# Stick-breaking scores of two heads in two PSUM banks, the recurrence's chain in one bank, and its bonus by one 128x128 product per pair of heads

## The chip, the cores and the metric

One core of one Trainium2 chip runs the whole kernel in a single launch. The metric is the device time of one execution in microseconds (us). A time is compared as the median of several runs; before the change this is 1360.16 us (three runs, 1359.88 to 1361.38). The profile is of one further execution.

The engines are named as in the profile: PE is TensorE (matrix products; PEld are its weight loads), DVE is VectorE, ACT is ScalarE, POOL is GpSimd, SP issues most of the DMAs.

## The reference, cut to what matters

The program computes two transformer blocks on a sequence of 512 tokens with 1024 features. The change lies in the first block's mixing layer, which has two parts of 8 heads with 64 features each. The second half of the first block (a routed mixture of 32 experts) and the second block (attention with windows) are not touched.

```python
# stick-breaking attention, by blocks of 128 queries
z = einsum('bhqd,bhkd->bhqk', qb, kb) * scale          # keys 0 .. end of the block
log_rest = where(strict, log_sigmoid(-z), 0.0)
suffix = cumsum(log_rest, reverse=True) - log_rest
weights = where(strict, exp(log_sigmoid(z) + suffix), 0.0)
outs.append(einsum('bhqk,bhkd->bhqd', weights, vb))
...
# RWKV-7 recurrence, one step per token, per head
state = state * w + (state @ -kk) (kk * a)^T + v k^T
out = state @ r
...
bonus = sum(r_h * k_h * r_k, axis=-1, keepdims=True) * v_h
out = (group_norm(out) + bonus) * g
```

## The kernel before, in words

Most tensors of the mixing layer hold the 64 features of two heads in 128 partitions and the 512 tokens in columns. So a "pair" p (0 to 3) is two heads, and a half hf (0 or 1) is two pairs. The dense projections (`fm`, `vjob`, `wo_mm`; lines 213 to 215) are products of split weights: high part, low part and the cross term, each 128x512 or 128x256.

The recurrence is done by chunks of 64 tokens (8 chunks, `NCH`). `rw_dense(hf)` projects and prepares a half; `rwkv(hf)` runs `chunks` (products `xt` inside a chunk), `inverse` (a triangular inverse on DVE, common to the two pairs), `front_a` and `front_b` (transposes, then the matrices Rt and Mt of each chunk), `chain(p)` and `rest(p, po)` (normalisation, the bonus, the gate).

`chain(p)` has two parts. First come products that need no state: for each chunk and head one into the bank `po` (line 678) and one into the bank `pst` (line 681). Then DVE turns `pst` into the start values St (line 685). After that there are the steps: for chunk c the product Mt x St goes into `pst` (line 691), DVE makes the next state St of it (line 692), and the product Rt x St is accumulated on top of what lies in `po` (line 694). At the end ACT copies `po` into O (line 703), and `rest` works on O.

The bonus is computed in two products. `bonus()` (line 509) sums r*k*r_k over the features of each head with the four-column matrix `hrk` (line 513, tile `bsp`, 4x512), and DVE copies the sums into `nb` (line 514). Later `front_b` spreads the sums over the 64 features with the constant `hT` (line 659, tile `pbn`), and DVE multiplies by v into `bvo` (line 661).

The stick-breaking part is `sb(p)`. For each query block i (0 to 3, with N = 128(i+1) keys) and head h: `s0` makes the scores (line 786, tile `sbz`, K = 64 rows of the array, since a head has 64 features), two sigmoids on ACT (788, 790), masks on POOL (793), a running product on DVE (797) and a product (798); `s1` transposes the weights on PE (806, tile `sbw`) and ACT copies them (808); `s2` multiplies by the values (818, tile `sbo`). The heads go one after the other, and the score tile has one bank, `pw`.

PSUM has eight banks here: two of the tag `pa` (dense products), two of the tag `pb` (taken in turn by almost everything else), and one each of `pw`, `so`, `po` and `pst`. A product into a bank waits until the engine that read the previous contents is done.

The order of the work is set in two steps. The program is written as generators: `blend` and `mix` interleave the recurrence (`mixing`) with a `filler` (value projections, the second half's `rw_dense`, then for each pair the query and key projections and `sb`, and the first part of the output projection `wo`) by tables of estimated costs (`CR`, `SW`, `SU`). Then a scheduler of the language lays out each engine's queue, within limits, by its own estimates. Each engine executes its queue in that order, so an instruction that waits holds all behind it.

## Time and profile before

| | |
|---|---|
| median of the runs | 1360.16 us (1359.88 to 1361.38) |
| the profiled execution, its own time | 1356.27 us |
| its span, first to last instruction | 1354.6 us |
| PE busy | 1268.5 us (94%) |
| DVE busy | 726.2 us (54%) |
| ACT busy | 482.2 us (36%) |
| POOL busy | 233.2 us (17%) |
| mean granted TensorE clock | 0.959 |

Times in the profile are us from the start of the span. "Busy" counts the time in which an engine has an instruction; products are pipelined, so consecutive ones overlap in the rows and what one costs is the distance from its start to the start of the next. [...] The mixing layer fills the span up to about 440 us, the choice of experts goes to 476 us, the experts to about 740 us, and the second block the rest.

### The profile page before, as it was taken

Reading aid. Unit: us, or ns where it says so; the run is one execution under the profiler, and the core shown is the slowest. Engines: PE = TensorE matmul, PEld = TensorE weight load, DVE = VectorE, ACT = ScalarE, POOL = GpSimd, SP = SyncE. Lnnn points to the kernel's source line nnn. Section 1 sums busy time; section 2 is a strip of 40 time slices with the busy share of each in tenths; the row PEclk is TensorE's granted clock in tenths of the full one; section 3 lists DMA queues with packets and bytes.
Section 4 is the critical chain, followed back from the end, with each engine's and each line's share of the span. In section 5 each row is a group of like instructions: output and inputs, shape, how many; then the busy total and the mean of one; then the engine's idle time right before and its main releaser. Section 6 shows DMA issues by size and latency. Waiting matters only on the chain.

```text
span 1354.6 us, 22340 instructions
## 1 busy us (share of the span) xinstructions
PE 1268.5 (94%) x9018; PEld 984.4 (73%) x9018; DVE 726.2 (54%) x1654; ACT 482.2 (36%) x1003; POOL 233.2 (17%) x318
## 2 busy tenths in 40 slices
PE   7999999999989599999996899999899999999998
PEld 5778765667567355555554888888899887888888
DVE  6468566866556524443446546666544457422362
ACT  5424432544313111111113355557344564322231
POOL 2230152322420311111001322211032100000000
PEclk9979999989789699999999799999999999999999
DMA  5211100011428699999950331203321132322232
GB/s 187 74 47 63 48 32 32 32 63 48 140 78 328 227 403 372 406 397 417 401 202 1 120 106 63 86 33 99 93 89 68 53 106 64 124 93 79 93 130 74
DMA packets 41820, 188.79 MB, mean 139 GB/s; under 512 B 10887, under 2 KB 13353, under 8 KB 24560
## 3 DMA queue, kind: packets, MB, share of 16 engines
q1 hardware_dynamic: 30800, 173.93, 33.7%
q0 software_dynamic: 4448, 10.87, 2.8%
q10 hardware_dynamic: 6464, 2.52, 0.8%
q8 instruction: 73, 1.20, 0.4%
q14 instruction: 35, 0.29, 0.1%
HBM read 183.54 MB, written 7.95 MB: 141 GB/s over the span
## 4 chain that ended last, share of the span: by engine, by line
PE 50%; issue 7%; ACT 3%; DVE 2%; DMA 1%; POOL 1%; DVEq 0%; ACTq 0%; POOLq 0%
PE tm L213 7%; PE tm L214 6%; PE tm L215 6%; PE gu L1232 5%; PE fm L215 4%; PE fm L213 4%; PE fm L214 4%; PE pd L1253 3%; PE cb L1268 3%; PE az L1544 2%; ACT Pb L1555 1%; PE pbT L1761 1%; PE qT L1502 1%; PE oa L1643 1%; PE paT L1629 1%
## 5 line engine op out<-in xcount | busy, mean ns | idle before, releaser
L213 PE MATMUL tm<-wh,ah 128*128 128x256 f32 x800 | 231.1, 289 | 5.3 <-ACT vb L1669 5.3
L215 PE MATMUL tm<-wh,al 128*128 128x256 f32 x800 | 226.7, 284 | 0.0
L214 PE MATMUL tm<-wl,ah 128*128 128x256 f32 x800 | 226.4, 283 | 0.3 <-DVE wl L205 0.3
L205 DVE TENSOR_TENSOR wl<-w,wh 128x1024 fp32r<-128x1024 f32 (+1 forms) x124 | 144.2, 1164 | 147.8 <-ACT wh L204 147.6
L204 ACT ACTIVATE wh<-w 128x1024 fp32r<-128x1024 f32 (+1 forms) x124 | 124.2, 1002 | 275.6 <-PE tm L214 93.2
L213 PEld LDWEIGHTS tm<-wh,ah 128*128 128x128 f32 x800 | 151.6, 189 | 12.2 <-ACT vb L1669 5.5
L214 PEld LDWEIGHTS tm<-wl,ah 128*128 128x128 f32 x800 | 151.8, 190 | 0.8 <-DVE wl L205 0.6
L215 PEld LDWEIGHTS tm<-wh,al 128*128 128x128 f32 x800 | 151.3, 189 | 1.1 <-issue 1.0
L280 POOL TENSOR_TENSOR qss<-qss,nhalf 128x4 f32<-128x4 f32 x60 | 63.7, 1075 | 198.7 <-DVE qss L275 198.5
L213 PE MATMUL u<-xh,wh 128*128 128x512 f32 x176 | 75.8, 431 | 4.6 <-ACT xh L365 4.1
L1272 DVE TENSOR_TENSOR hres<-hres,cb 128x512 f32<-128x512 f32 x72 | 48.9, 686 | 54.3 <-PE cb L1268 54.2
L214 PE MATMUL u<-xl,wh 128*128 128x512 f32 x176 | 75.0, 426 | 1.8 <-DVE xl L366 1.8
L213 PE MATMUL fm<-ah,wh 128*128 128x512 f32 x192 | 76.0, 396 | 0.1
L215 PE MATMUL fm<-ah,wl 128*128 128x512 f32 x192 | 75.9, 395 | 0.1
L214 PE MATMUL fm<-al,wh 128*128 128x512 f32 x192 | 75.9, 395 | 0.0
L215 PE MATMUL u<-xh,wl 128*128 128x512 f32 x176 | 73.3, 416 | 1.5 <-DVE wl L205 1.5
L1253 PE MATMUL pd<-ed,hTs 128*64 128x512 f32 x256 | 62.0, 600 | 2.3 <-ACT hTs L1245 2.1
L1232 PE MATMUL gu<-eg,xgT 128*64 128x256 f32 x512 | 63.1, 384 | 0.3 <-DVE xgT L1224 0.3
L1268 PE MATMUL cb<-yh,C 128*128 128x512 f32 x128 | 55.9, 437 | 6.0 <-DVE C L1258 4.9
L1232 PE MATMUL gu<-eu,xgT 128*64 128x256 f32 x512 | 61.2, 380 | 0.0
L1235 ACT ACTIVATE hm<-gu 128x256 f32<-128x256 f32 x16 | 6.2, 384 | 148.5 <-PE hT L1243 102.2
L1232 PEld LDWEIGHTS gu<-eg,xgT 128*64 128x64 f32 x512 | 37.6, 138 | 21.8 <-issue 4.9
(404 smaller groups left out, 2527.8 us busy)
## 6 DMA issues: line engine op xcount, KB each, us to landing
w<-in_w_dram SPq DMA_DIRECT2D x33, 1024.0 KB, 4.8
eg<-in_exp_w_gate_dram SPq DMA_DIRECT2D x32, 1024.0 KB, 11.4
eu<-in_exp_w_up_dram SPq DMA_DIRECT2D x32, 1024.0 KB, 17.0
ed<-in_exp_w_down_dram SPq DMA_DIRECT2D x32, 1024.0 KB, 9.9
w<-in_wi_dram SPq DMA_DIRECT2D x22, 512.0 KB, 3.5
w<-in_wo_dram SPq DMA_DIRECT2D x8, 512.0 KB, 3.4
w<-in_wo_dram SPq DMA_DIRECT2D x4, 1024.0 KB, 4.9
xT<-in_xT_dram SPq DMA_DIRECT2D x4, 512.0 KB, 6.4
```

Of the source, the lines that this page charges most:

```text
L204: i = nc.scalar.activation(hi, src, AF.Copy)
L205: j = nc.vector.tensor_tensor(lo, src, hi.bitcast(F), op=OP.subtract)
L213: mm(out, lh, rh, start=first, stop=False)
L214: mm(out, lh, rl, start=False, stop=False)
L215: mm(out, ll, rh, start=False, stop=last)
L280: nc.gpsimd.tensor_tensor(out, out, e if len(out.shape) == 2 else e.rearrange("p (a b) -> p a b", b=out.shape[2]), op=OP.pow)
L1232: nc.tensor.matmul(ph[es, c0:c0 + 256], xt[:, c, es], EW[n, 2 * q + k][:, c, :], start=(c == 0), stop=(c == 7))
L1253: nc.tensor.matmul(pd[es, :], hT[:, c, es], EW["d", 2 * q + k][:, c, hf * 512:(hf + 1) * 512], start=(c == 0), stop=(c == 1))
L1268: nc.tensor.matmul(ps, C[:, i * 128:(i + 1) * 128], y[:, hf * 512:(hf + 1) * 512], start=(n == 0), stop=(n == 2 * len(ys) - 1))
L1272: tt(hv, hv, ps, op=OP.add)
L1502: nc.tensor.transpose(ps[:, i * 128:(i + 1) * 128], sc[:, i, :], eye)
L1544: nc.tensor.matmul(pz[j][:, off:off + k1 - k0], qt[rows, i * 128:(i + 1) * 128], kt[rows, k0:k1], start=True, stop=True)
```

## The change

1. Scores: with h = 0, `s0` now issues the score products of both heads, one into the bank `pw` and one into the bank `pst`. Head 0 uses rows 0 to 63 of the array and head 1 rows 64 to 127. The rest of `s0` is as before, head by head.
2. The chain: the state-free products go into two tiles of the tag `pb`, first all `pst` products (line 677 of the changed kernel) and then all `pso` products (line 683), and ACT copies `pso` into O at once. In the steps, both Mt x St (columns 0 to 63, line 691) and Rt x St (columns of chunk c, line 694) go into the one bank `po`, without accumulation. At the end DVE adds `po` to O (line 696). So `chain` no longer uses the bank `pst`.
3. The bonus: a 128x128 block matrix of ones, `own`, is filled by POOL at the start (three memsets). For each pair POOL scales it with r_k (line 513, tile `ownrk`), one product (line 515, tile `bsp`, now 128x512) sums over the features and spreads the sums at once, and DVE multiplies by v into `bvo` (line 517), in `bonus()` and no longer in `front_b`. The products `pbn`, the copies `nb`, the four `hrk` instructions and the constant `hT` (256 of 976 columns of the first block of constants) are gone.

```diff
-for _n, _w in (("xmask", 128), ("hind", 8), ("hT", 256), ("e0", 520), ("eye2", 64), ("ustr", 128), ("tok", 8), ("i16", 8), ("io512", 512)):
+for _n, _w in (("xmask", 128), ("hind", 8), ("e0", 520), ("eye2", 64), ("ustr", 128), ("tok", 8), ("i16", 8), ("io512", 512)):
...
-    hT = np.zeros((4, 2, 128), np.float32)
-            hT[2 * p + h, p, 64 * h:64 * h + 64] = 1
-    put("hT", hT.reshape(4, 256))
...
-        nb = [a_("nb", [4, 512], bufs=2) for _ in range(2)]
...
-        hrk = a_("hrk", [128, 4, 4])
-        for p in range(4):
-            ts(hrk[:, p, :], hind[:, p % 2, :], self.pc("rw_r_k", p), None, op0=OP.mult)
+
+        own = a_("own", [128, 128])
+        nc.gpsimd.memset(own, 0.0)
+        for h in range(2):
+            nc.gpsimd.memset(own[64 * h:64 * h + 64, 64 * h:64 * h + 64], 1.0)
+        bvs = [None] * 4
...
             def bonus():
-                bsp = self.pb("bsp")
                 for q in range(2):
-                    nc.tensor.matmul(bsp[0:4, :], hrk[:, 2 * hf + q, :], kt[q], start=(q == 0), stop=(q == 1))
-                nc.vector.tensor_copy(nb[hf][0:4, :], bsp[0:4, :])
+                    p = 2 * hf + q
+                    z = el("ownrk", [128, 128])
+                    nc.gpsimd.tensor_tensor(z, own, self.pc("rw_r_k", p).to_broadcast([128, 128]), op=OP.mult)
+                    bsp = self.pb("bsp")
+                    nc.tensor.matmul(bsp, z, kt[q], start=True, stop=True)
+                    bvs[p] = self.t(PB, "bvo", [128, 512], bufs=4)
+                    tt(ch(bvs[p]), ch(bsp), rqv[p][:, :, 128:192], op=OP.mult)
             late_bonus.append(bonus)
             if hf == 0:
                 jobs += [(lambda: first, fm(0, lora_w)[1]), fm(1, lora_g)]
...
                         nc.tensor.matmul(p1[hs, c * 64:(c + 1) * 64], W[0:64, c, h, 0:64], XT[0:64, pp, c, h, 0:64], start=True, stop=True)
                 tt(Rt, p1.rearrange("p (c t) -> p c t", t=64), rqv[p][:, :, 0:64], op=OP.add)
                 yield CR[hf][3]
-                pbn = self.pb("pbn")
-                nc.tensor.matmul(pbn, self.c("hT")[0:4, pp * 128:(pp + 1) * 128], nb[hf][0:4, :], start=True, stop=True)
-                bv = rw_("bvo", [128, 512], bufs=2)
-                tt(ch(bv), ch(pbn), rqv[p][:, :, 128:192], op=OP.mult)
-                tiles[p] += [Rt, Mt, bv]
-                yield CR[hf][3]
+                tiles[p] += [Rt, Mt]
                 if p % 2:
                     self.half = hf + 1
             def chain(p):
                 pp = p % 2
-                BK, W, Rt, Mt, _ = tiles[p]
+                BK, W, Rt, Mt = tiles[p]
                 St = cc_("St")
-                po = self.p1("po", "po")
-                pst = self.p1("pst", "pst")
+                O = dd_("O", [128, NCH, 64])
                 heads = [slice(64 * h, 64 * h + 64) for h in range(2)]
-                for c in range(NCH):
-                    o = slice(c * 64, (c + 1) * 64)
-                    for h, hs in enumerate(heads):
-                        nc.tensor.matmul(po[hs, o], XT[:, pp, c, h, 0:64], W[:, c, h, 64:128], start=(c == 0), stop=False)
-                    if c < NCH - 1:
-                        for h, hs in enumerate(heads):
-                            nc.tensor.matmul(pst[hs, o], BK[:, c, hs], W[:, c, h, 64:128], start=True, stop=True)
-                    if c == 3:
-                        yield CR[hf][4]
                 n = NCH - 1
+                pst = self.pb("pst")
+                for c in range(n):
+                    for hs in heads:
+                        nc.tensor.matmul(pst[hs, c * 64:(c + 1) * 64], BK[:, c, hs], W[:, c, hs.start // 64, 64:128], start=True, stop=True)
                 tt(St[:, 1:NCH, :], ch(pst)[:, 0:n, :], pcd[:, p, 0:n, None].to_broadcast([128, n, 64]), op=OP.mult)
                 yield CR[hf][4]
+                pso = self.pb("pso")
+                for c in range(NCH):
+                    for h, hs in enumerate(heads):
+                        nc.tensor.matmul(pso[hs, c * 64:(c + 1) * 64], XT[:, pp, c, h, 0:64], W[:, c, h, 64:128], start=True, stop=True)
+                nc.scalar.activation(O, ch(pso), AF.Copy)
+                yield CR[hf][4]
+                po = self.p1("po", "po")
                 for c in range(1, NCH):
-                    o = slice(c * 64, (c + 1) * 64)
                     if c < n:
                         for hs in heads:
-                            nc.tensor.matmul(pst[hs, o], Mt[hs, c, :], St[hs, c, :], start=True, stop=True)
-                        stt(St[:, c + 1, :], pst[:, o], pcd[:, p, c:c + 1], St[:, c + 1, :], op0=OP.mult, op1=OP.add)
+                            nc.tensor.matmul(po[hs, 0:64], Mt[hs, c, :], St[hs, c, :], start=True, stop=True)
+                        stt(St[:, c + 1, :], po[:, 0:64], pcd[:, p, c:c + 1], St[:, c + 1, :], op0=OP.mult, op1=OP.add)
                     for hs in heads:
-                        nc.tensor.matmul(po[hs, o], Rt[hs, c, :], St[hs, c, :], start=False, stop=(c == n))
+                        nc.tensor.matmul(po[hs, c * 64:(c + 1) * 64], Rt[hs, c, :], St[hs, c, :], start=True, stop=True)
                     yield CR[hf][4]
-                return po
-            def rest(p, po):
+                tt(O[:, 1:NCH, :], O[:, 1:NCH, :], ch(po)[:, 1:NCH, :], op=OP.add)
+                return O
+            def rest(p, O):
                 pp = p % 2
-                O = dd_("O", [128, NCH, 64])
-                nc.scalar.activation(O, po.rearrange("p (c t) -> p c t", t=64), AF.Copy)
                 st = a_("gst", [128, NCH], bufs=2)
                 nc.vector.tensor_reduce(st, O, axis=AX.X, op=OP.add)
                 ts(st, st, 1.0 / 64, None, op0=OP.mult)
...
-                bv = tiles[p][4]
+                bv = bvs[p]
...
             def s0(i, h):
                 N = 128 * (i + 1)
-                hs = slice(64 * h, 64 * h + 64)
-                pz = self.p1("sbz", "pw")
-                nc.tensor.matmul(pz[:, 0:N], qk[p // 2][hs, 2 * (p % 2), i * 128:(i + 1) * 128], qk[p // 2][hs, 2 * (p % 2) + 1, 0:N], start=True, stop=True)
+                if h == 0:
+                    st["z"] = [self.p1("sbz", b) for b in ("pw", "pst")]
+                    for z, r in zip(st["z"], (slice(0, 64), slice(64, 128))):
+                        nc.tensor.matmul(z[:, 0:N], qk[p // 2][r, 2 * (p % 2), i * 128:(i + 1) * 128], qk[p // 2][r, 2 * (p % 2) + 1, 0:N], start=True, stop=True)
+                pz = st["z"][h]
                 sm = s2_("sm")
                 nc.scalar.activation(sm[:, 0:N], pz[:, 0:N], AF.Sigmoid, scale=-0.125)
                 sp = s2_("sp")
```

The change moves instructions, since it changes the code's order and the scheduler lays the queues out again. Three places follow. A "[waits ...]" names the engines whose progress the row needs.

PE, the score products of pair 1, blocks 0 to 2 (`u` are dense projections, `sbw` transposes of the weights, `sbo` products with the values, `obT` transposes of pair 0's output). Before:

```order
L786 MATMUL sbz<-qk 128x128 [waits DVE_49]
L214 MATMUL u<-xl,wh 128x512
...
L786 MATMUL sbz<-qk 128x128 [waits Activation_49]
...
L786 MATMUL sbz<-qk 128x256 [waits Activation_49]
L806 MATMUL sbw<-ident,sp 128x128 [waits DVE_49,Activation_49]
L818 MATMUL sbo<-vs,wt 128x64 [waits PE_49]
...
L786 MATMUL sbz<-qk 128x256 [waits Activation_49]
```

Now:

```order
L786 MATMUL sbz<-qk 128x128 [waits DVE_49]
L786 MATMUL sbz<-qk 128x128
L212 MATMUL u<-xh,wl 128x512
...
L786 MATMUL sbz<-qk 128x256 [waits Activation_49] x2
L807 MATMUL sbw<-ident,sp 128x128 [waits DVE_49,Activation_49]
L819 MATMUL sbo<-vs,wt 128x64 [waits PE_49]
L210 MATMUL u<-xh,wh 128x512
L786 MATMUL sbz<-qk 128x384 [waits Activation_49]
L819 MATMUL sbo<-vs,wt 128x64 [waits Activation_49]
L786 MATMUL sbz<-qk 128x384 [waits Activation_49]
```

The two products of 128 and of 256 columns stand side by side now; between those of 384 columns another product still stands. Over the four pairs of heads, 10 of the 16 pairs of products are neighbours: four of 128 columns, three of 256, none of 384, three of 512.

PE, two steps of the chain of pair 3 (`wo` is the output projection). Before:

```order
L691 MATMUL pst<-St,Mt 64x64 [waits DVE_49]
L691 MATMUL pst<-St,Mt 64x64
L694 MATMUL po<-St,Rt 64x64 x2
L214 MATMUL wo<-wl,oh 128x512
L215 MATMUL wo<-wh,ol 128x512
L213 MATMUL wo<-wh,oh 128x512
L818 MATMUL sbo<-vs,wt 128x64 [waits Activation_49]
L818 MATMUL sbo<-vs,wt 128x64 x3
L214 MATMUL wo<-wl,oh 128x512
L691 MATMUL pst<-St,Mt 64x64 [waits DVE_49]
```

Now:

```order
L691 MATMUL po<-St,Mt 64x64 x2
L211 MATMUL wo<-wl,oh 128x512
L212 MATMUL wo<-wh,ol 128x512
L210 MATMUL wo<-wh,oh 128x512
L694 MATMUL po<-St,Rt 64x64 [waits DVE_49]
L694 MATMUL po<-St,Rt 64x64
L691 MATMUL po<-St,Mt 64x64 x2
L211 MATMUL wo<-wl,oh 128x512
```

The wait for DVE stood at Mt and stands now at Rt, and the other products stand between Mt and Rt of one step instead of between Rt of one step and Mt of the next.

POOL, the end of the mixing layer: the normalisation of pair 3's recurrence (`O`, `gs`) and of pair 3's stick-breaking output (`sbs`, `on`). Before:

```order
L707 TENSOR_TENSOR O<-O,gst 128x512 [waits DVE_49,Activation_49]
L280 TENSOR_TENSOR sbs<-sbs,nhalf 128x8 [waits DVE_49]
L829 TENSOR_TENSOR on<-on,sbs 128x512 [waits PE_49,Activation_49,Pool_49]
L280 TENSOR_TENSOR gs_3463<-gs_3463,nhalf 128x8 [waits DVE_49]
L716 TENSOR_TENSOR O<-O,gs_3463 128x512 [waits Activation_49,Pool_49]
```

Now:

```order
L277 TENSOR_TENSOR sbs<-sbs,nhalf 128x8 [waits DVE_49]
L830 TENSOR_TENSOR on<-on,sbs 128x512 [waits Activation_49,Pool_49]
L705 TENSOR_TENSOR O<-O,gst 128x512 [waits DVE_49]
L277 TENSOR_TENSOR gs_3452<-gs_3452,nhalf 128x8 [waits DVE_49]
L714 TENSOR_TENSOR O<-O,gs_3452 128x512 [waits Activation_49,Pool_49]
```

The two instructions of the stick-breaking output moved ahead of the recurrence's first one.

## Rows read from the trace of the kernel before

**Rows 1.** Four stretches: length, busy time of each engine, PEclk, DMA share, GB/s.

```profile
220.00:356.00 136.00, 127.49 (x1074) 90.64 (x1071) 98.17 (x185) 64.38 (x137) 46.65 (x105) 0.94 0.16 53
356.00:374.00 18.00, 18.00 (x100) 10.44 (x101) 6.98 (x14) 3.26 (x6) 2.13 (x5) 0.53 0.47 165
374.00:440.00 66.00, 59.74 (x337) 47.76 (x337) 40.80 (x62) 17.01 (x26) 9.31 (x9) 0.95 0.56 208
476.00:680.00 204.00, 201.95 (x1317) 116.90 (x1315) 80.29 (x135) 26.39 (x51) 21.45 (x22) 1.00 0.97 399
```

**Rows 2.** Timeline, PE (start, duration, what): three score products, each with its successor.

```profile
340.92 0.48 PE L786 MATMUL sbz<-qk 64*128 64x128 f32 x2
341.33 0.33 PE L681 MATMUL pst<-W,bk 128*64 128x64 f32 x2
...
303.11 0.70 PE L786 MATMUL sbz<-qk 64*128 64x256 f32 x2
303.74 0.43 PE L633 MATMUL wu<-W,T 64*64 64x128 f32 x4
...
320.72 1.12 PE L786 MATMUL sbz<-qk 64*128 64x512 f32 x2
321.77 0.44 PE L806 MATMUL sbw<-ident,sp 128*128 128x128 f32 x2
```

**Rows 3.** Timeline, PE: two products on different array rows and banks.

```profile
159.00 0.69 PE L473 MATMUL yw<-lora,w2a 64*128 64x512 f32 x1
159.01 0.69 PE L475 MATMUL ya<-lora,w2a 64*128 64x512 f32 x1
...
159.53 0.59 PE L473 MATMUL yw<-lora,w2a 64*128 64x512 f32 x1
...
160.06 0.28 PE L678 MATMUL po<-W,hres 128*64 128x64 f32 x2
```

**Rows 4.** Timeline, PE: the bonus's products, each with the row behind.

```profile
92.23 1.88 PE L513 MATMUL bsp<-kt,hrk 128*4 128x512 f32 x4
94.04 0.37 PE L541 MATMUL xt<-rqv,bk 64*128 64x128 f32 x1
...
155.07 1.12 PE L659 MATMUL pbn<-nb,cstxmask 4*128 4x512 f32 x2
156.12 0.34 PE L678 MATMUL po<-W,hres 128*64 128x64 f32 x4
...
359.36 2.07 PE L659 MATMUL pbn<-nb,cstxmask 4*128 4x512 f32 x2
361.36 0.47 PE L818 MATMUL sbo<-vs,wt 128*128 128x64 f32 x1
```

**Rows 5.** Single lines of DVE and ACT: count, ns min/median/max.

```profile
L514 DVE COPY nb<-bsp x2: 671/675/679, 94.4 to 205.9; 4x512 f32<-4x512 f32 x2
...
L661 DVE TENSOR_TENSOR bvo<-pbn,rqv x4: 690/690/693, 156.2 to 361.5; 128x512 f32<-128x512 f32 x4
...
L685 DVE TENSOR_TENSOR St<-pst,pcd x4: 611/617/625, 161.8 to 362.7; 128x448 f32<-128x448 f32 x4
...
L703 ACT ACTIVATE O<-po x4: 593/595/599, 178.9 to 378.1; 128x512 f32<-128x512 f32 x4
```

**Rows 6.** The chain: line 692 on DVE; one step, PE then DVE.

```profile
L692 DVE SCALAR_TENSOR_TENSOR St<-pst,pcd,St x24: 257/282/288, 165.7 to 376.7; 128x64 f32<-128x64 f32 x24
...
329.69 0.33 PE L691 MATMUL pst<-St,Mt 64*64 64x64 f32 x4
...
330.07 0.28 DVE L692 SCALAR_TENSOR_TENSOR St<-pst,pcd,St 128x64 f32<-128x64 f32 x1 [1.25 <-PE pst L691]
```

**Rows 7.** Timeline, POOL and then PE, end of the mixing layer.

```profile
383.84 1.64 POOL L280 TENSOR_TENSOR sbs<-sbs,nhalf 128x8 f32<-128x8 f32 x1 [3.01 <-DVE sbs L275]
385.56 1.04 POOL L829 TENSOR_TENSOR on<-on,sbs 128x512 f32<-128x512 f32 x1
...
389.38 1.98 PE L722 MATMUL oT<-ident,O 64*64 64x64 f32 x32 [3.77 <-POOL O L716]
```

## The prediction

> **What bounds the kernel now.** I read the page of the profile first: PE is busy 94% of the span and is most of the chain that ended last. An average over stages says little, so next came busy time by stretches [rows 1]. In the stretch of the stick-breaking work, 220 to 356 us, PE is busy for 127.5 of 136.0 us, while DVE is at 98 and ACT at 64: PE sets the pace, with 8.5 us in which it waits for something. In the last part of the mixing layer, 374 to 440 us, it is busy for 59.7 of 66 us. [...] Behind the mixing layer, in the experts (476 to 680 us), PE is busy for 201.95 of 204 us. The change touches nothing there, so what the mixing layer gains should reach the end: the expert loads start when buffers of the mixing layer come free, and move with it.
>
> So the question is how many us of PE's queue the change takes out before 440 us, and what it puts on paths that PE waits for.
>
> **The scores.** A product of scores alone occupies PE from its start to the next start: 0.41 us for 128 columns, 0.63 for 256, 1.05 for 512 [rows 2] (0.84 for 384, by the same slope). It uses 64 of the array's 128 rows. What two such products cost together when they use different rows and different banks is already in this kernel: lines 473 and 475, 512 columns each, start 0.01 us apart, and their second passes too (each of these products is two instructions). Both are done in 160.06 - 159.00 = 1.06 us, the price of one [rows 3]. So where two score products are neighbours in PE's queue, one of them is free; where another product stands between, nothing is gained. Ten pairs are neighbours: 4 x 0.41 + 3 x 0.63 + 3 x 1.05 = 6.7 us. In two of the three pairs of 512 columns the second product has a wait for ACT of its own; if it is late there, those two give nothing, and the sum is 4.6. I take 6.7, because ACT is busy for less than half of this stretch [rows 1].
>
> **The bonus.** The four products `pbn` go: 1.05 us each at the full clock, and the last, in the slow stretch, 2.00 [rows 4]: 3 x 1.05 + 2.00 = 5.2 us. The four products `bsp` before take about 0.9 us each (92.23 to 94.04 for two) [rows 4]; the new ones are also four products with 512 columns, so at most at the price of a `pbn`, 0.15 us more each: 0.6 us. DVE loses two copies of 0.675 us; its four products by v of 0.69 us stay, but now two of them stand in `bonus()` where one copy stood, ahead of the inverse [rows 5]: 0.7 us later there, once per half. During the inverse PE has projections to do, so I count half of the 1.4 us, with 0 and 1.4 as ends. POOL's four multiplications of 128x128 are not in the trace. Each is bounded by nothing and by the 1.04 us of a 128x512 one [rows 7]; POOL is busy for a third of the stretch [rows 1], so I count nothing, with 2 us as the other end (two of them stand ahead of work that PE's `xt` products wait for). The constants' shorter load and the three memsets at the start: nothing.
>
> **The chain.** The number of products is the same. ACT's copy of O (0.595 us) leaves the end of the chain, and DVE's addition takes its place (448 columns; line 685 has that shape, 0.617 us) [rows 5]: no difference. What changes is the waiting. A step is Mt x St on PE, then 0.28 us on DVE, and from PE's start to DVE's end it takes at least 330.07 + 0.28 - 329.69 = 0.66 us [rows 6]. Before, Rt of the same step and then projections covered this; now the projections alone do. In the changed order, 22 of the 24 steps have other products between Mt and Rt worth 0.6 us or more by starts in the timeline, so I count 0.5 us. Splitting Mt from Rt makes one more change of the array's shape per chain, and taking `pst` and `pso` each in one go makes fewer. The price of such a change comes from rows 2: from 128 to 512 columns the cost grows by 0.64 us for 384 columns, so 128 columns are 0.21 us, and 0.20 of the 0.41 is the visit itself, about 0.1 us on either side. In PE's whole queue of the mixing layer there are 15 fewer changes of shape than before, while the terms above already contain 28 (two for each of ten score products and four `pbn`). So 13 come in anew elsewhere: +1.3 us.
>
> [...] By the rows a step's reading by DVE is covered by other products, in whatever bank it lies [rows 6]. [...]
>
> **The end of the mixing layer.** PE waits 3.77 us there for the normalised O of pair 3, which POOL finishes [rows 7]. In POOL's new order two instructions of the stick-breaking output, 1.64 + 1.04 = 2.7 us, come ahead of this path, while the last values are done earlier in PE's queue. I count 0.5 us, between 0 and 2.7.
>
> **The sum.** Gains 6.7 + 5.2 = 11.9. Losses 0.6 + 0.7 + 0.5 + 1.3 + 0.5 = 3.6. That leaves 8.3 us on PE's path. Of the freed time some turns into longer waits in the stretch where PE already waits for 8.5 us; I round to 8. The profiled execution has a span of 1354.6 us and a time of 1356.3, so 1.7 us lie around the span; it is 3.9 us under the median of the runs. The same 8 us off the median: 1360.2 - 8.2 = **1352.0 us** (and about 1348 for an execution like the profiled one). With the ends of the terms: best, no losses but 1.3, 10.6 us, so 1349.6; worst, 4.6 + 5.2 - (0.6 + 1.4 + 2 + 2 + 1.3 + 2.7) = -0.2, so no change.
>
> **The rivals.**
>
> *The score pairs give nothing* (either they do not overlap, or ACT, POOL and DVE behind them set the pace, so that PE only waits longer). For: 8.5 us of waits are there already, and the masks on POOL and the running products on DVE stay in their old number. Against: rows 3. Then 11.9 - 6.7 - 3.6 = 1.6 us of gain stay, and with the two changes of shape per free pair still paid, about 1; with fewer losses up to 4. Time 1357.5, half of this case within 0.2%. Chance 0.18.
>
> *The clock follows.* The 18 us at half clock cost about 9 us. With denser work the stretch could stay at full clock: 1352 - 9 = 1343. For: the slow pieces before stand where many small products and waits stand. Chance 0.10. The opposite, a new slow piece that takes the gain back: 1361, chance 0.06.
>
> *The one bank decides, and it is slower.* If in each of the 24 steps PE stands still for the whole 0.66 us, that is 15.8 us, and the four additions of 0.62 us at the chains' ends 2.5 us. Gains of 8.3 against 18.3: 10 us slower, 1370; with half of the steps uncovered 1362. It becomes slower than before from about 0.25 us per step on. For: the scheduler's estimates set the order, and products on the chip can be shorter than it thinks. Against: before, PE's queue stood after the same kind of cover, and DVE was done 0.3 to 1 us ahead of the next Mt in most steps. Chance 0.14.
>
> **How the numbers follow.** The forecast has the rest, 0.52; its own range is 1348 to 1356. A measurement of this kernel can tell some 0.2% (2.7 us) from no change. Faster: 0.52 + 0.10 + half of 0.18 = 0.71. Same: 0.09 + 0.06 = 0.15. Slower: 0.14. The range for 8 in 10 takes in the clock's gain and the case without pairs, and leaves out most of the slower case: 1343 to 1362.
>
> **What would show it.** In the profile after: score products of two heads that start 0.01 us apart, and both done in the price of one; no `pbn`; line 692 at 0.28 us and no idle time of PE ahead of line 694; the state-free products in two blocks; the idle time ahead of `oT` still 3 to 6 us; the end of the mixing layer, and with it the experts' start, some 8 us earlier, with the stretches behind unchanged. The forecast is wrong if neighbours do not overlap, if idle time ahead of line 694 or of the transposes `sbw` has grown by several us, or if the pieces at half clock before 480 us differ from before by more than 10 us in sum.

## The result and the profile after

The changed kernel takes 1340.35 us (median of four runs, 1338.84 to 1345.2) against 1360.02; the ratio is 0.9858, interval 0.984 to 0.9876. That is 19.7 us less where 8 were forecast: 7.7 us below the forecast's own range (1348 to 1356) and 2.7 us below the wide one (1343 to 1362). Four executions over 1.5% above the fastest of their kernel (1360.97 and 1368.02 us in e12, 1361.06 and 1368.38 us in e14) are slow ones and stand outside all ratios, medians and averages below. The profiled execution of the changed kernel, 1345.2 us, is the longest of the four, as that of before (1356.3) is a short one: the two profiles are only 11 us apart.

Four stretches of the changed kernel answer to [rows 1] (length, busy time of PE, PEld, DVE, ACT and POOL with counts, PEclk, DMA share, GB/s); each is moved to where the same work lies now. The second line is a fifth stretch, around a piece at half clock.

```profile
212.00:349.00 137.00, 121.54 (x1041) 89.80 (x1038) 101.28 (x189) 61.93 (x133) 45.67 (x102) 0.94 0.16 54
338.00:345.00 7.00, 6.27 (x49) 4.80 (x49) 4.53 (x7) 0.89 (x4) 3.49 (x10) 0.57 0.11 45
349.00:374.00 25.00, 24.23 (x251) 18.26 (x246) 16.27 (x29) 8.27 (x17) 6.87 (x13) 1.00 0.51 190
374.00:428.00 54.00, 48.46 (x262) 39.10 (x262) 33.01 (x49) 14.04 (x21) 5.61 (x6) 0.94 0.61 226
464.00:668.00 204.00, 201.96 (x1315) 116.95 (x1313) 80.56 (x136) 26.38 (x51) 21.44 (x22) 1.00 0.97 399
```

The experts are as before, 201.96 of 204 us; the mixing layer ends some 12 us earlier. In the stretch of the scores PE waits for 15.5 us instead of 8.5, and the piece at half clock behind it (17.00 of the 18 us in [rows 1]) is gone; another, of 7 us, stands at 337.

The score pairs and the new bonus on PE, in the timeline (start, duration, what):

```profile
238.33 1.13 PE L786 MATMUL sbz<-qk 64*128 64x512 f32 x4
239.39 0.55 PE L807 MATMUL sbw<-ident,sp 128*128 128x128 f32 x3
...
93.24 1.88 PE L515 MATMUL bsp<-kt,ownrk 128*128 128x512 f32 x4
95.05 1.16 PE L544 MATMUL xt<-rqv,bk 64*128 64x128 f32 x8
```

Two score products of 512 columns (four instructions) take 239.39 - 238.33 = 1.06 us together, one alone took 1.05 [rows 2]; the new `bsp` takes 0.9 us, as the old one [rows 4].

From the distances of PE's starts I made a ledger for each profile, up to the first product behind the mixing layer (427.7 us before, 415.5 after). It has three parts: work at the price of the full clock (time at half clock counted half, as eight products `xt` that take 1.09 us at 197.93 us in before, at the full clock, take 2.00 at 200.33 us, at the half), what the half clock adds, and idle time over 0.15 us.

| us | before | after |
|---|---|---|
| scores | 23.4 | 16.6 |
| bonus | 7.7 | 3.7 |
| chain | 18.7 | 18.6 |
| other products | 314.2 | 314.5 |
| added by the half clock | 30.7 | 22.6 |
| idle | 33.0 | 39.4 |

Work is 10.5 us less, waits are 6.4 us more, and 8.1 us come from the clock. The waits of PE from 219 to 352 us (us in total, times, longest), first before, then after:

```profile
PE sbw L806 <- DVE sp L798: 3.2, 4, 1.7
PE bkT L590 <- DVE zo L724: 2.1, 1, 2.1
PE sbw L806 <- ACT oT L837: 1.0, 1, 1.0
```

```profile
PE sbw L807 <- DVE sp L799: 7.2, 6, 2.4
PE oT L720 <- POOL O L714: 4.0, 1, 4.0
PE oT L720 <- POOL I L797: 1.7, 1, 1.7
PE sbw L807 <- ACT sp L791: 1.5, 1, 1.5
```

The granted clock in the pieces at half clock between 190 and 400 us (the same columns), first before, 48 us in all, then after, 27 us:

```profile
199.00:206.00 7.00, 7.00 (x23) 3.05 (x23) 1.63 (x4) 0.00 (x0) 1.19 (x1) 0.51 0.00 0
233.00:243.00 10.00, 9.73 (x27) 6.29 (x27) 7.26 (x20) 3.31 (x10) 3.13 (x11) 0.51 0.01 3
281.00:288.00 7.00, 7.00 (x21) 4.61 (x20) 5.00 (x6) 2.17 (x4) 1.54 (x3) 0.51 0.49 160
356.00:373.00 17.00, 17.00 (x94) 9.93 (x93) 6.44 (x12) 3.26 (x6) 2.13 (x5) 0.50 0.50 175
387.00:394.00 7.00, 4.62 (x37) 3.33 (x38) 0.81 (x1) 0.00 (x0) 3.51 (x3) 0.52 0.01 2
```

```profile
197.00:200.00 3.00, 2.85 (x34) 2.73 (x36) 1.32 (x3) 0.00 (x0) 2.92 (x3) 0.54 0.03 5
228.00:231.00 3.00, 3.00 (x9) 1.64 (x9) 2.97 (x5) 0.00 (x0) 1.41 (x2) 0.50 0.00 0
272.00:279.00 7.00, 6.33 (x21) 5.38 (x22) 6.75 (x8) 1.58 (x3) 2.58 (x3) 0.53 0.35 141
337.00:344.00 7.00, 5.27 (x42) 4.01 (x43) 3.94 (x7) 0.00 (x0) 4.15 (x10) 0.51 0.23 75
378.00:385.00 7.00, 6.19 (x40) 4.56 (x41) 1.71 (x3) 0.00 (x0) 2.02 (x2) 0.51 0.23 77
```

So the forecast's work is there and the clock, which it left as it was, has moved. One profile cannot price that, since it changes from execution to execution (114 to 145 us at half clock in those of before); the runs can, within limits.

### The profile page after: what moved, and what is told of

Its sections match the earlier page's. It is cut to its first block, busy times and chain, and to the rows that moved or that the text cites. A ratio compares the mean times of both kernels' runs of the same rounds, so it can differ in the third digit from the quotient of the medians.

```text
span 1343.5 us, 22311 instructions
## 1 busy us (share of the span) xinstructions
PE 1252.1 (93%) x9010; PEld 982.5 (73%) x9010; DVE 729.3 (54%) x1652; ACT 480.2 (36%) x1003; POOL 234.1 (17%) x325
## 4 chain that ended last, share of the span: by engine, by line
PE 53%; issue 7%; ACT 2%; DVE 2%; POOL 1%; DMA 1%; DVEq 0%; ACTq 0%; POOLq 0%
PE tm L210 7%; PE tm L212 7%; PE tm L211 7%; PE gu L1233 5%; PE fm L210 4%; PE fm L211 4%; PE fm L212 4%; PE pd L1254 3%; PE cb L1269 3%; PE az L1545 2%; PE pbT L1762 1%; PE qT L1503 1%; PE oa L1644 1%; PE paT L1630 1%; DMA fd<-znt 1%
## 5 line engine op out<-in xcount | busy, mean ns | idle before, releaser
L210 PE MATMUL u<-xh,wh 128*128 128x512 f32 x176 | 75.3, 428 | 4.5 <-ACT xh L361 4.0
```

The source lines that it names most:

```text
L210: mm(out, lh, rh, start=first, stop=False)
```

## How the runs are read

Each execution lists its span and mean granted clock. In the first two profiles the clock is at 1.00 or 0.50 in every stretch (111.0 us of before and 99.0 us of the changed kernel at 0.50), so I take 2 x span x (1 - clock) as the time at half clock of every execution. Within one kernel, a us more of it goes with 0.39 us more time (one slope through 194 executions, with a mean of its own for every kernel). With this slope each kernel's time is also given at 127 us of half clock: what the program itself is worth, without the clock. The last column is span x clock, the measure that most expectations below use; it counts time at half clock as half.

| kernel | executions | median us | us at half clock, mean (range) | time at 127 us | span x clock |
|---|---|---|---|---|---|
| before (e2 and beside all runs) | 85 | 1361.8 | 128 (114 to 145) | 1361.7 | 1296.3 |
| changed (e1, e15, e17 and the result) | 21 | 1342.9 | 102 (86 to 119) | 1353.6 | 1291.1 |
| bonus alone (e5, e12) | 9 | 1341.0 | 92 (80 to 130) | 1356.8 | 1295.4 |
| chain alone (e6) | 12 | 1357.7 | 122 (103 to 142) | 1361.5 | 1296.8 |
| chain and scores (e7) | 4 | 1342.8 | 99 (91 to 105) | 1353.8 | 1291.7 |
| chain and bonus (e4) | 6 | 1349.3 | 101 (86 to 114) | 1357.8 | 1295.5 |
| the same, Mt in its own bank (e8) | 4 | 1348.7 | 108 (102 to 113) | 1356.1 | 1293.0 |
| changed, pairs on the same rows (e3) | 6 | 1344.0 | 107 (96 to 133) | 1354.1 | 1291.0 |
| changed, each score in its turn (e10) | 6 | 1346.7 | 109 (86 to 133) | 1354.9 | 1291.7 |
| changed, last block in turn (e11) | 6 | 1346.0 | 101 (86 to 113) | 1356.0 | 1293.6 |
| before, bonus on full rows (e9) | 6 | 1355.7 | 115 (108 to 122) | 1360.0 | 1296.1 |
| changed, products behind a wait (e13) | 6 | 1339.3 | 79 (72 to 88) | 1357.1 | 1297.1 |
| bonus alone, the same (e14) | 5 | 1342.7 | 88 (83 to 100) | 1359.4 | 1298.5 |
| changed, in another bank (e16) | 6 | 1341.5 | 85 (80 to 91) | 1358.2 | 1297.5 |
| before, in another bank (e18) | 12 | 1358.2 | 112 (103 to 117) | 1364.2 | 1300.6 |

The standard error of a mean in the last two columns is 0.1 to 1.1 us. The slope is a larger doubt where two kernels differ much in their time at half clock: in the kernels with twelve or more executions it is 0.22 to 0.41. So a difference over 10 us of half clock or more is given by both columns, and only kernels with nearly the same half clock (the changed one, e3, e4, e7, e8, e10 and e11, 99 to 109 us) compare safely.

By the slope the change is worth 1361.7 - 1353.6 = 8.1 us of its own, and 26 us less at half clock bring another 0.39 x 26 = 10.2. By span x clock it is 5.2 and 13.1 us. The ledgers stand nearer to the second: work and idle time together are 396.5 us in two profiles of the kernel before and 390.7 in four of the changed one, 5.8 us less. By all three the clock's part is the larger.

## The experiments

**Both kernels again (e1, e2, e15, e17), no edit.**

> The changed kernel without an edit, to have a second profile of it and more times beside the kernel before. In the two profiles at hand the change gains 12.2 us up to the end of the mixing layer: the work on PE, with stretches at half clock counted at the full clock's price, is 10.6 us less, the idle time of PE 6.5 us more, and 8 us come from 16 us less time at half clock. The medians differ by 19.7 us, so 7 to 8 us are not in these two profiles. Clock theory: the work is as fixed as the program, and the rest of the difference is granted clock; then in a second profile the work at full-clock price is again 353.5 us within 1 us, and where the time is 5 us less than 1345.2, the time at half clock is some 10 us less. Waits theory: time at half clock is the same, and idle time of PE differs by 5 us. Time expected 1340, ratio 0.986.

> The kernel before without an edit, for a second profile of it. Its first profiled execution took 1356.3 us where the median is 1360. Clock theory: work at full-clock price up to the end of the mixing layer 364 us within 1 us, idle time of PE near 29.6 us, and the difference of 4 us in 8 us more at half clock (61 us in the first profile). Waits theory: the half-clock time is 61 us again and idle time is longer. Ratio 1.000.

> The changed kernel without an edit for the third time, beside the two above on the same chip: 1343 (nine runs so far, 1338.8 to 1349.5), 100 us at half clock.

> The changed kernel without an edit, beside the two others on the same chip: 1342 (fifteen runs so far, 1338.8 to 1349.5), 100 us at half clock.

Measured: the changed kernel 1346.13 (e1), 1342.04 (e15) and 1346.17 us (e17); ratios 0.9875 (0.9847 to 0.9904), 0.9862 (0.9837 to 0.9887) and 0.9859 (0.9828 to 0.989). Before: 1361.21, ratio 1.0004 (0.9986 to 1.0022). In the second profiles the work in the ledger is 352.0 us (changed) and 363.0 (before), within 1.5 of the first ones, and the half clock adds 31.0 and 36.4 instead of 22.6 and 30.7. Idle time is 36.6 to 39.4 us in the four profiles of the changed kernel and 33.0 and 33.6 in the two of before. As the clock theory said, the program's work holds, and the granted clock makes most of the spread.

**The parts (e5, e6, e7, e4).** The bonus alone is the kernel before with the diff's third part:

```diff
-                    nc.tensor.matmul(bsp[0:4, :], hrk[:, 2 * hf + q, :], kt[q], start=(q == 0), stop=(q == 1))
-                nc.vector.tensor_copy(nb[hf][0:4, :], bsp[0:4, :])
+                    nc.tensor.matmul(bsp, z, kt[q], start=True, stop=True)
+                    tt(ch(bvs[p]), ch(bsp), rqv[p][:, :, 128:192], op=OP.mult)
...
-                nc.tensor.matmul(pbn, self.c("hT")[0:4, pp * 128:(pp + 1) * 128], nb[hf][0:4, :], start=True, stop=True)
```

> The kernel before with the change's bonus alone. In the runs so far the span times the mean granted clock (the span if all of it ran at the full clock, so a measure of work and waits) is 1296.4 us for the kernel before and 1291.8 for the changed one, and the time at half clock (two times the span times what the mean clock lacks to 1) is 127 and 100 us: of some 17 us of gain 13 are the clock's. The chain and the bonus together, with the scores as before, have 1295.5 and 101: the clock's part is theirs. Theory bonus: the bonus brings the clock's part; then about 101 us at half clock, span times clock 1292 to 1293 (3.9 us less work in the ledger of the profiles), median 1345. Theory chain: 127 us at half clock, the same 1292 to 1293, median 1357.

The chain alone is the kernel before with the second part:

```diff
-                            nc.tensor.matmul(pst[hs, o], Mt[hs, c, :], St[hs, c, :], start=True, stop=True)
+                            nc.tensor.matmul(po[hs, 0:64], Mt[hs, c, :], St[hs, c, :], start=True, stop=True)
```

> The kernel before with the change's chain alone (the bank that it leaves stays empty). Theory bonus: 127 us at half clock, span times clock 1296 to 1299 (the chain's products cost the same, waits may grow by up to 3 us), median 1361. Theory chain: 101 us at half clock, the same 1296 to 1299, median 1349. If neither has it alone, both lie near 115 us.

Chain and scores are the first two parts, with the old `bonus()` and `pbn`:

> The changed kernel with the bonus as before: chain and scores are as in the change. By the ledger the work is 3.9 us more than in the changed kernel: span times clock 1295 to 1296. Theory bonus: 127 us at half clock, median 1360. Theory chain: 100 us at half clock, median 1348.

Chain and bonus have the scores as before:

```diff
-                    st["z"] = [self.p1("sbz", b) for b in ("pw", "pst")]
...
+                pz = self.p1("sbz", "pw")
```

> The changed kernel with the scores as before: each head's product in its own turn, both through the one score bank, and the other bank left empty. What remains of the change is the chain and the bonus. By the prediction's sum these two give 5.2 - 3.6 = 1.6 us: 1358, ratio to before 0.999. If the scores' second bank and the overlap are all of the gain, no better than before: 1360. If most of the 19.7 us comes from chain and bonus, by a better order or the clock: 1345 to 1350, ratio 0.99.

Measured: 1340.94 (ratio 0.9842, 0.9829 to 0.9854), 1357.7 (0.9983, 0.9958 to 1.0009), 1342.81 (0.9854, 0.9839 to 0.9868) and 1349.26 (0.9895, 0.986 to 0.993). Neither theory holds: the bonus alone takes half-clock time away (80 to 88 us in the five executions of e5, 83 to 130 in four of e12), and so do chain and scores without it. Without the clock the chain alone is worth nothing (0.2 us more or 0.5 less). The bonus alone is worth 4.9 us by the slope but only 0.9 by span x clock, which misses the 1292 to 1293 that were expected. In the ledgers of e5 and e12 its work is some 4 us less and the idle time some 4 us more. Chain and scores are worth 7.9 or 4.6 us. On top of these, at the same half clock, the bonus adds 0.2 (+-0.5) or 0.6 (+-0.8): most of its 4 us less work on PE has turned into waits there too.

**The bank of the chain (e8),** beside e4:

```diff
-                            nc.tensor.matmul(po[hs, 0:64], Mt[hs, c, :], St[hs, c, :], start=True, stop=True)
+                            nc.tensor.matmul(pm[hs, 0:64], Mt[hs, c, :], St[hs, c, :], start=True, stop=True)
```

> Chain and bonus of the change with the scores as before, and in the chain the product Mt x St in a bank of its own (the one that the scores leave empty), so that DVE's reading of it and the product Rt x St do not share a bank; beside the run with one bank for both, which had 1349.3 us, 1295.5 for span times clock and 101 us at half clock. Rule theory (one bank holds the next product until DVE is done): PE's waits ahead of Rt go, 24 steps by up to 0.66 us, so span times clock down by 2 us or more. Theory of the prediction (other products cover the reading): the same within 1.5 us. In both the clock's part stays near 101 us if it hangs on the chain's products and not on their banks.

Measured: 1348.69 against 1349.26. Without the clock it is 1.8 us (+-0.8) better, and 2.5 (+-0.8) by span x clock, the size that the rule theory asked for. Its mechanism explains less: in e4's timeline PE waits ahead of Rt for 0.9 us in all, in e8's not at all there, but for 0.6 us ahead of Mt. The scheduler also laid PE's queue out otherwise in many places, and in e8's ledger the work is some 5 us less. So the one bank may cost something, at most a sixth of the third rival's 15.8 us; what of the 1.8 to 2.5 us is the bank and what the order stays open.

**The score pairs (e3, e10, e11).** Both products read the same rows, which leaves the scores of head 1 out:

```diff
-                    for z, r in zip(st["z"], (slice(0, 64), slice(64, 128))):
+                    for z, r in zip(st["z"], (slice(0, 64), slice(0, 64))):
```

> The changed kernel, in which the second product of a score pair reads head 0's rows of the array and of the data once more, so the scores of head 1 are left out (those of head 0 stand in both banks). Each engine's order and all sizes are as in the changed kernel; only the overlap on different rows of the array is gone. Overlap theory: the ten pairs that are neighbours lose what they gained, 6.7 us in all (the scores went from 27.0 to 17.5 us in the profiles, of which 2.7 us are the clock), so 1347, ratio to the changed kernel 1.005, if the clock's pieces stay. Clock theory: PE is busier with the same products, the time at half clock may move either way by 10 us, and the time lies anywhere from 1342 to 1352. If the overlap is worth nothing: 1340.

Measured: 1344.04 (0.9863, 0.9838 to 0.9889); at equal half clock 1354.1, within 0.5 (+-0.5) of the changed kernel. The overlap is gone (timeline of PE):

```profile
239.65 1.45 PE L786 MATMUL sbz<-qk 64*128 64x512 f32 x3
241.03 0.55 PE L807 MATMUL sbw<-ident,sp 128*128 128x128 f32 x3
```

With its first instruction at 239.12 us this pair takes 1.91 us instead of 1.06, and the scores are some 4.5 us more in the ledger. But the waits shrink by as much: for `sp` to 4.2 us, all of PE's between 219 and 360 us to 10.9 from 15.3 (219 to 352). The profiled execution of e3 has much time at half clock, but that is not the reason: in all four profiles of the changed kernel, one of which (e1) has 20 us at half clock at 321 us as e3 has at 317, the waits for `sp` are 7.2 to 7.4 us. The overlap saves time on PE in which PE would wait for DVE.

```profile
PE sbw L807 <- DVE sp L799: 4.2, 5, 1.4
```

Each product in its own turn, still in two banks (six neighbours instead of ten):

```diff
+                pz = self.p1("sbz", ("pw", "pst")[h])
```

> The changed kernel with two banks for the scores, but each head's product issued in the head's own turn, as before the change. Six pairs are neighbours in PE's queue (four of 128 columns, two of 256), against ten in the changed kernel. With the scores in one bank and chain and bonus as changed, span times clock is 1295.5; side by side in two banks 1291.8; with the overlap taken away but the order kept 1291.0. Bank theory (the gain is that the second head's scores need not wait until ACT has read the first's): 1291 to 1293. Early theory (the gain is that both scores are there early): 1295. Clock: 95 to 110 us at half clock in either.

Measured: 1346.66 (0.9891, 0.9849 to 0.9934), without the clock 1354.9 against 1357.8 with one bank (e4) and 1353.6 with the pairs side by side. So of the 4.2 us of the scores' part the second bank is 2.9 (+-1.0), most of it; span x clock, 1291.7, lies where the bank theory put it. The waits of ACT from 219 to 352 us show it, with one bank (e4) and with two in turn (e10):

```profile
ACT sm L786 <- PE sbz L784: 23.1, 17, 6.9
```

```profile
ACT sm L786 <- PE sbz L784: 6.0, 6, 2.7
```

The last block of queries alone in turn:

```diff
+                        if i < 3 or g == h:
```

> The changed kernel, with the scores side by side for the first three blocks of queries and in each head's own turn for the fourth (512 columns), in the two banks. In two profiles of the changed kernel PE waits 2.4 us at 270 us for the transposes behind the two products of 512 columns of pair 1, and 2 us on a piece of 6.8 us at half clock begins. Waits theory (a wait of PE starts a piece at half clock): the wait shrinks, since other products stand between, and the piece at 272 us goes; 7 us less at half clock (93), span times clock up by the lost overlap of at most 3 us, median 1341 to 1343. Otherwise the piece stays where it is: 1343 to 1346.

Measured: 1346.04 (0.9878, 0.9851 to 0.9905), 101 us at half clock: the piece at 272 us is gone in its profile, but the mean over the runs is not lower, and the time lies above the 1341 to 1343 expected. That a shorter wait brings less time at half clock is not shown by it.

**The rows of one product (e9).** In the kernel before, `pbn` with all 128 rows, 124 of them zero:

```diff
-        nb = [a_("nb", [4, 512], bufs=2) for _ in range(2)]
+        nb = [a_("nb", [128, 512], bufs=2) for _ in range(2)]; [nc.gpsimd.memset(z, 0.0) for z in nb]
...
-                nc.tensor.matmul(pbn, self.c("hT")[0:4, pp * 128:(pp + 1) * 128], nb[hf][0:4, :], start=True, stop=True)
+                nc.tensor.matmul(pbn, self.c("hT")[:, pp * 128:(pp + 1) * 128], nb[hf], start=True, stop=True)
```

> The kernel before with one edit: the product that spreads the bonus (4 rows of sums by a 4x128 matrix) is done on all 128 rows of the array, 124 of them zero on both sides; POOL clears the two tiles of sums at the start. Columns, results, banks and each engine's order stay as before, so span times clock stays at 1296.4 within 1 us. In both profiles of the kernel before, the piece at half clock at 199 us begins right behind such a product and two waits of PE, and the long one at 356 us (17 to 20 us) holds another. Rows theory (products on few rows of the array count for the clock like waits): the piece at 199 us goes and the one at 356 us shrinks, so 10 to 20 us less at half clock than 127, median 1351 to 1357. Order theory (the bonus moves the clock's pieces by moving waits, and the rows have no part): 127 us at half clock, 1362.

Measured: 1355.71, ratio 0.9947 (0.9925 to 0.9969); 115 us at half clock against 129 beside it. PE's, DVE's and ACT's orders are those of before. Before, the clock fell at 199 us behind the first product shown here (the timeline of before, then that of e9 with its clock between 199 and 206 us and between 356 and 387):

```profile
196.88 1.12 PE L659 MATMUL pbn<-nb,cstxmask 4*128 4x512 f32 x2 [0.68 <-DVE Mt L649]
```

```profile
199.40 1.13 PE L659 MATMUL pbn<-nb,cstxmask 128*128 128x512 f32 x2 [0.67 <-DVE Mt L649]
```

```profile
199.00:206.00 7.00, 6.60 (x37) 3.75 (x38) 4.40 (x8) 0.00 (x0) 3.62 (x3) 1.00 0.00 0
356.00:387.00 31.00, 31.00 (x153) 21.88 (x153) 12.87 (x23) 7.04 (x12) 3.17 (x6) 0.51 0.32 116
```

The same product with the same wait ahead, and no fall at 199 us. By the runs (108 to 122 us at half clock, against 114 to 145 before) the products on 4 rows are part of what held the clock down, about 5 us of time. The profile alone does not show it: the long piece at 356 us is longer, and in all this execution has 122 us at half clock, where the two profiled ones of before have 111 and 120. Pieces at 197 to 199 us also stand in kernels without such products (3.4 us in the changed one, 6.8 in e8), and POOL's two memsets at the start, the other part of the edit, were not tried alone.

**The bonus alone, again (e12), no edit.**

> The kernel before with the change's bonus alone, once more, for a second profile and to see whether its time holds: it had 1340.9 us, span times clock 1296.0, 85 us at half clock. If the clock's part is the program's own: 1339 to 1343 and 80 to 92 us. If it was that chip's or that hour's: 1345 to 1355 and 100 us or more.

Measured: 1343.18 (1339.46 to 1358.86), ratio 0.988 (0.9835 to 0.9925), 83 to 130 us at half clock; the time of e5 did not hold. One program, two lengths of the same piece; in both, PE waits 3.90 us for POOL ahead of `oT` just before it. First e5, then e12, whose profiled execution is the one of 1358.86 us:

```profile
331.00:341.00 10.00, 8.12 (x62) 6.28 (x62) 4.37 (x7) 1.53 (x6) 4.83 (x12) 0.52 0.17 54
```

```profile
337.00:381.00 44.00, 44.00 (x233) 29.29 (x231) 18.94 (x31) 10.69 (x25) 6.72 (x22) 0.50 0.23 84
```

**Products at a wait (e13, e14, e16, e18).** In every profile without such products PE waits 3.0 to 4.3 us between 70 and 80 us, ahead of the tile `rnb`, and a piece of 10 to 20 us at half clock follows. Three products into the bank of `rnb`:

```diff
                 rnb = self.pb("rnb")
+                for _ in range(3 if p == 1 else 0): nc.tensor.matmul(rnb, eye, L, start=True, stop=True)
```

> The changed kernel with three products of 128x512 more, of the constant identity with a tile that is ready, into the tile rnb of the second pair just ahead of its own products, which overwrite them. PE waits 3.06 us there for ACT (at 74 us, in every profile), and 2 to 4 us later a piece of 10 to 20 us at half clock begins. Three such products take about 3.15 us, so they lie in the wait. Waits theory (a wait of PE brings the half clock behind it): the piece at 78 us goes, 10 to 14 us less at half clock than the changed kernel in the same call, and at 0.40 us a piece (the slope within one kernel, over all runs) 4 to 5.5 us faster. Other theory (the clock's pieces have another cause): the same time at half clock, 0 to 0.5 us slower.

> The kernel with the change's bonus alone, with the same three products in the same wait. Waits theory: 10 us less at half clock than the 101 us of its eleven runs, and 4 us less time at the same mix of executions, median 1337 to 1340. Other theory: 1341, with the same wide range up to 1368.

Four, into the bank `po`, which is free then:

```diff
+                if p == 1:
+                    fz = self.p1("fz", "po")
+                    for _ in range(4): nc.tensor.matmul(ch(fz), eye, rqv[p][:, :, 128:192], start=True, stop=True)
                 rnb = self.pb("rnb")
```

> The changed kernel with four products of 128x512 more ahead of the tile rnb of the second pair, but into a bank that nothing holds at that time, so that they need not wait as those of the first trial did (there the three products stood behind the wait, since their bank was the one waited for; PE waited 4.3 us and 72 to 88 us ran at half clock). Four products of about 1.05 us lie in the wait of 3.06 us and take up to 1.2 us more. Waits theory: the wait goes, the piece of 14 us at 78 us goes with it, 80 to 86 us at half clock and 1.2 us more work: median 1336 to 1338. If only work behind a wait brings the clock back, and the wait itself has no part: the piece stays, 99 us, 1342 to 1343.

> The kernel before with the same four products in the same wait: none of the change is in it. Waits theory: 127 us at half clock becomes 107 to 114, since its piece at 76 us has 14 to 20 us, and at 0.42 us a piece with 1.2 us more work the median is 1355 to 1358. Otherwise 1361 to 1363.

Measured: e13 1339.27 (1335.21 to 1340.74; ratio 0.9834, 0.9806 to 0.9862), with the changed kernel beside it at 1342.04 (1340.98 to 1343.2). e14 1342.68 (0.9881, 0.9848 to 0.9913), and its long executions stay. e16 1341.46 (1339.5 to 1344.31) beside 1346.17 (1341.5 to 1348.32). e18 1358.21, ratio 0.9962 (0.9945 to 0.998). The gains lie between the theories for e13 (2.8 us where 4 to 5.5 were expected) and e16 (above the 1336 to 1338 expected); e18 is at the edge of its range and e14 misses its own. The changed kernel without the products (e17), then e13, then e16: first PE's timeline, then two stretches.

```profile
78.11 1.61 PE L482 MATMUL rnb<-ident,rnt 128*64 128x128 f32 x16 [3.06 <-ACT sg L476]
```

```profile
78.70:92.20 13.50, 13.50 (x60) 11.83 (x57) 7.05 (x10) 3.31 (x4) 6.67 (x8) 0.50 0.04 13
```

```profile
76.06 5.34 PE L480 MATMUL rnb<-lora,ident 128*128 128x512 f32 x6 [4.32 <-ACT sg L476]
```

```profile
78.70:92.20 13.50, 13.18 (x86) 9.86 (x85) 7.77 (x11) 1.97 (x3) 6.24 (x8) 0.91 0.01 1
```

```profile
75.77 5.14 PE L481 MATMUL fz<-rqv,ident 128*128 128x512 f32 x8 [2.76 <-DVE rqv L414]
```

```profile
78.70:92.20 13.50, 12.99 (x93) 10.29 (x93) 7.85 (x11) 2.54 (x4) 6.25 (x8) 1.00 0.00 1
```

No trial filled the wait: in e13 the bank was what PE waited for, in e16 the operand came late from DVE, and the products stand behind the wait. The clock still falls there (it was 0.50 from 75.3 to 78.7 us in both), but it is back after 3 to 7 us instead of 14. Products on all 128 rows behind a wait cost 2.5 to 4.6 us (the time at 127 us, against the kernel without them) and brought back 7 to 9 us of clock in e13, e16 and e18 (19 to 22 us less at half clock than the kernel without them beside it), and next to nothing in e14. Only 7 to 10 us of the 19 and 22 in e13 and e16 are this piece. The rest is in other pieces: in e13's profile the one of 6.8 us at 54 us, which lies ahead of the products, is gone as well. Whether the edit reaches those, and how, is open. e13 is faster than both kernels, in each of its six runs than in any run of the changed kernel beside it. That a filled wait keeps the clock up was not tried in any run.

## Why the prediction was wrong

The step that failed is the clock. The sum took the pieces at half clock as they were, so it put the change of the clock at nothing; "the clock follows" stood among the rivals with a chance of 0.10 and for one stretch only, with 9 us. It was the larger part: 10.2 of 18.3 us (means) by the slope, 13.1 by span x clock. Two signs that the prediction named as showing it wrong came true. The pieces before 480 us fell from 85 to 68 us in the profiles, by more than 10 (85 and 96 us in two profiles before, 68, 72, 82 and 89 in four after). And PE's waits ahead of the transposes `sbw` grew from 4.4 to 8.7 us between 219 and 352 us.

- **The sum without the clock.** 8 us predicted; 5.2 (span x clock), 5.8 (ledgers) or 8.1 (slope) measured. The work is right: 11.9 - 0.6 - 1.3 = 10.0 us predicted, 10.5 in the first ledgers. The waits are too low: 0.7 + 0.5 + 0.5 + 0.3 = 2.0 us predicted, 6.4 in the first ledgers and 4.9 as the mean of all. Where the total comes near 8, that is in part luck.
- **Scores.** 6.7 us on PE predicted, 6.8 in the ledger. But e3 has the same time without the overlap (1354.1 against 1353.6 us at equal half clock): the rival "the score pairs give nothing" is right on the overlap. There is a gain all the same, and e10 shows where most of it comes from: the second bank, in which the second head's scores need not wait until ACT has read the first's (2.9 of 4.2 us; ACT's waits for the scores fall from 23.1 us in e4 to 6.0 us in e10). The prediction had not priced it.
- **Bonus.** 5.2 - 0.6 - 0.7 = 3.9 us predicted; the ledger has 4.0 us less work. Of these 0.9 to 4.9 us reach the time alone, and 0.2 to 0.6 on top of the rest. `bsp` costs 0.9 us, not more.
- **Chain.** 0.5 us of loss for the waits and 1.3 for changes of shape predicted; nothing measured alone (0.2 us gained or 0.5 lost), and the other products are 0.3 us dearer in the ledger. Line 692 takes 0.28 us as before. The rival of the one bank, 10 us slower, is off by its cover: in the changed kernel's PE queue only one wait ahead of Rt is over 0.5 us (0.55).
- **The rounding.** 0.3 us stood for gains that turn into longer waits; among the waits this is the term that was sized wrong. Between 219 and 352 us PE waits 7.2 us for DVE ahead of `sbw` (3.2 before) and 5.7 us for POOL ahead of `oT` (0.3 before).
- **The end.** 1.95 us ahead of `oT` and 2.24 us ahead of `wo` shortly before; 5.1 us were there before for both. No loss of 0.5 us, and the 1.95 us lie outside the 3 to 6 that the prediction named.

What makes the time at half clock less in the change is settled in part. In 19 profiles I counted 106 pieces between 60 and 420 us: 93 begin within 7 us of a wait of PE of 0.87 us or more, 10 of shorter waits, 3 of none. Only 15% of the time at the full clock there lies so close behind such a wait, so this is more than chance; but about a third of these waits (57 of the 173 that begin at the full clock) have no piece behind them. Shown by an edit: the four products on 4 rows, which the bonus takes out, bring 14 us of half clock in the kernel before (e9); and full-row products behind a wait shorten the piece (from 78.7 to 92.2 us the clock is 0.91 in e13, 1.00 in e16 and 0.95 in e18; without them it is 0.50 in e17, and 0.51 from 76 to 90 us in before). Not shown: that the change's 26 us less are the sum of such parts, and that the scores in two banks act by moving waits. Open: why one program has the piece at 331 us in 10 us of one execution and in 44 of another.

## What to carry to other kernels

Where pieces at half clock stand in the profile, they are a term of the sum with a range of its own: list them before, and ask of every edit which waits (here 93 of 106 pieces begin behind one of 0.87 us or more) and few-row products (here 14 us of half clock, e9) it puts ahead of them. Compare kernels also at equal time at half clock; otherwise the clock is taken for the edit. Where their half clock differs much, say how much of the answer hangs on the slope. Here an overlap on PE that saved 0.85 us on a pair was worth nothing where PE waited right behind it (e3, within 0.5 us of the changed kernel), and a second bank for a tile that ACT reads was worth 2.9 us (e10).

## What was unexpected of the hardware

PE was busy for 44.00 of 44 us at a granted clock of 0.50 (e12, 337 to 381 us), in 228 instructions of which 139 (61%) use 64 rows or fewer; at the full clock, between 60 and 420 us of the same profile, it is 48%. This piece too begins behind a wait (3.90 us, for POOL), but 44 us in which PE did not stand idle did not end it. In e9 the rows of a product changed the clock (1.00 from 199 to 206 us, 0.51 before) and its time on PE did not (1.13 us, 1.12 before). What else counts, no run here settles.
